# Two-layer hybrid decoder trunk: earlier weight sums, merge sums on VectorE, and first-layer Gram products and bonus later in program order

## The chip, the cores and the metric

The kernel runs on 1 core of one Trainium2 chip. The metric is device time in microseconds (us), one launch from start to end. Five engines take part: PE (TensorE, with PEld for its weight loads), DVE (VectorE), ACT (ScalarE), POOL (GpSimd) and SP, which only issues transfers. POOL and ACT also issue transfers from their own queues.

## The reference, cut to what matters

Two layers, each with a token mixer of three parallel branches merged by gates, and a gated MLP with a causal convolution of width 3. SEQ is 512, D_MODEL 1024, D_FF 2816.

```
h = rmsnorm(x, norm1_g[l]);  p = h @ w_in[l]
y_rw  = rwkv7_branch(...)       # 8 heads of 64, state recurrence, plus
                                # y + sum(r * k * r_k) * v       ("bonus")
y_ret = retention_branch(...);  y_sg = sgu_branch(...)
proj  = einsum('bsgc,gcd->bsgd', [y_rw, y_ret, y_sg], w_branch[l])
gates = sigmoid(gate_logits)                            # 3 branches
x = x + sum(gates * proj, axis=2) @ w_out[l]            # the merge
u = rmsnorm(x, norm2_g[l]) @ ffn_w_up[l]                # up projection
c = conv_b + sum_j conv_w[j] * shifted(u, j)
x = x + (silu(gate) * val) @ ffn_w_down[l]              # down projection
```

## The kernel before, in words

Activations lie transposed: a tile is 128 channels by 512 tokens. Every large product is made of three matmuls (`mm3`, L194). Each operand is split into a high part `hi` (a CAST by ACT) and a low part `lo` (a subtraction by DVE), and lo·hi, hi·hi and hi·lo are added up in one PSUM bank. Weights come as 128x512 tiles `wr` from DRAM through the SP queue and are split in `part`: ACT writes `wh` or `sh` (L175), DVE writes `wl` or `sl` (L178). The two names stand for two buffer pools and nothing else. `plan` is the list of weight tiles in the order of use, and `part` runs some tiles ahead of PE. PSUM has four banks `acc` for the large products and four banks `sm` for the rest.

The order of the instructions on each engine is set by a scheduler, which runs its own timeline over the program as written and its priorities. Only what goes through `keep_in_program_order` keeps the order written. So writing code elsewhere may or may not move instructions.

A layer runs in these stages:

- **RWKV columns and blocks.** `cols3(m)` makes the k, r and v columns of block m (two heads) by PE, then DVE (L594, L597) and ACT (L596). `prep(m)` makes decays and the tiles `X`, `Y`, `bk` of the block: two small products `wus` (L637, L638) into `sm` banks, a chain over ACT and DVE, and then the Gram products, 64 small matmuls (L676, L679) into four `sm` banks. ACT copies these banks out to `Y` (L681) and `GB` (L680). `bonus(m)` multiplies r, k and r_k, splits the result, sums it over a head with two matmuls by `bonesR` (L693, L694) into an `sm` bank, and multiplies with v (L695).
- **Solve and recurrence.** `solve` inverts triangular blocks on DVE (L890 to L910) while PE runs the gate columns (`fill`), then PE takes the result (L918). The recurrence over 8 chunks follows, also between gate columns.
- **Merges.** `SEQ` is the written order of the stage. `merge(l, br, m, ...)` fetches a gate tile `gth` from DRAM through the POOL queue (L1148), multiplies the branch's output with `w_branch` on PE (12 matmuls), and DVE computes (gate + 1) times product (L1151), which frees the `acc` bank. For the second branch in `SEQ` (`2`) the sum with the first branch's tile is done by POOL (L1154). For the last (`1`) it is done by DVE (L1154), followed by a split for `wout`.
- **FFN.** Up projections, 44 columns c of 24 matmuls per layer: PE, DVE (`fu`, L1202), ACT (`cv`, L1204), DVE (L1205, L1206), and for a pair Silu and a product (`fth`). The down projection uses sums and differences of quarters of the weights. They are formed beside the up projections: `presum(l, c)` goes through `PRE[l]`, a table from the first column `at` to the quadruple q. In columns at to at+3 it fetches four tiles `pre` (L289, SP queue), in columns at+4 to at+7 DVE forms one sum each (L162), and POOL's queue stores it (L304). The down projection starts while the last columns end.

Of the kernel before, what the change touches and what calls it, by code (L numbers as in the profile page):

```python
# [23 lines left out]
FIRST = (12, 4, 0, 8)  # L24
FILL = (36, 2, 1)
KEPT = 6
PRE = {0: {4 + 4 * k: 2 + k for k in range(9)}, 1: {4: 0, 10: 1, 16: 2, 22: 3, 29: 4, 36: 6}}
RSUM = {(0, 3): (0, 0), (0, 10): (0, 1), (1, 3): (1, 8), (1, 10): (1, 10)}
NOW = ((1, 5), (1, 7), (1, 9))
SEQ = "0 H G G 0 S 0 U U G G 0 S 0 0 S 2 2 Y 0 0 2 1 2 1 2 1 2 1 2 1 2 1 1 1"  # L30
# [23 lines left out]
class Emit:  # L54
# [109 lines left out]
    def part(self, u):  # L164
        raw, n, pool = self.raws.pop(0), u[4], u[5]
        if type(raw) is tuple:
            raw = self.sumnow(raw)

        self.turn = (self.turn + 1) % 5 if pool in ("p", "q") else 4
        if pool is None or self.turn < 3:  # L170
            hi, lo = [self.wp.tile([128, 512], F32R, name=self.nm(t), tag=t, bufs=3) for t in ("wh", "wl")]
        else:
            hi, lo = [{"f": self.f, "r": self.r, "u": self.u, "p": self.u, "q": self.u}[pool](dt=F32R, n=t) for t in ("sh", "sl")]
        with self.tc.high_priority() if pool in (None, "p", "q") else nullcontext():
            self.kept(self.nc.scalar.copy(hi[:, :n], raw[:, :n]))  # L175
            if self.raws and type(self.raws[0]) is tuple:
                self.sumnow(self.raws[0])
            self.kept(self.nc.vector.tensor_tensor(lo[:, :n], raw[:, :n], hi[:, :n], op=SUB))  # L178
        self.parts.append((hi, lo))
        self.npart += 1  # L180
# [102 lines left out]
    def presum(self, l, c):  # L283

        for at, q in PRE[l].items():
            n = c - at
            if 0 <= n < 4:
                self.pre[l, q, n] = t = (self.f if at < 21 else self.u if l or at in (28, 36) else self.r)(n="pre")
                self.kept(self.nc.sync.dma_start(t, self.raw4(l, q, (1, 3, 0, 2)[n])))  # L289
            if 4 <= n < 8:  # L290
                b = [self.pre[l, q, k] for k in (2, 0, 3, 1)]
                p = (7, 5, 6, 4)[n - 4]
                t, i = self.sum4(b, p)
                self.kept(i)
                self.stores.append(((l, q), p, t))
                self.store4(n=1)
# [188 lines left out]
    def mixer(self, l, nst):  # L485
# [15 lines left out]
        sg, out = self.sgu_v(l), self.rwkv_out(l, *st)  # L501
# [12 lines left out]
        for step in SEQ.split():  # L514
            if step == "S":
                self.ret_pair(*next(rows))
            elif step == "G":
                ysg.append(self.sgu_out(len(ysg)))
            elif step == "H":
                self.ret_heads()  # L520
            elif step == "U":
                next(rest), next(rest)
            elif step == "Y":
                yret = self.ret_out()
            elif step == "0":
                mg.append(self.merge(l, 0, len(mg), yrw))
            elif step == "2":
                mg[m2] = self.merge(l, 2, m2, ysg, mg[m2])
                m2 += 1
            else:  # L530
                out.append(self.split(self.merge(l, 1, len(out), yret, mg[len(out)], self.nc.vector), self.f))
        return out

    def fillers(self, l):
# [33 lines left out]
    def rwkv(self, l, nst):  # L568
# [53 lines left out]
        X, Y, BK, Vf, bv = [], [], [], [], []  # L622
        kc, rc = [], []

        def cols3(m):
            kc.append(col(4 + m))
            rc.append(col(m))
            Vf.append(col(8 + m))

        def prep(m):  # L630


            k, r, v = kc[m], rc[m], Vf[m]
            ms = slice(m * 128, m * 128 + 128)
# [33 lines left out]
            V.tensor_tensor(f, f, cx[:, 0:7, 64], op=MUL)  # L668
            V.transpose(tha, ksq)
            V.tensor_reduce(pr[:, m], tha.rearrange("p (j r) -> p j r", r=32), axis=AX.X, op=ADD)  # L670
            for g in range(2):
                pB, pK = [self.sm((128, 4, 128)) for _ in range(2)]
                for j in range(4):
                    c = 4 * g + j
                    for h in range(2):
                        i = T.matmul(pK[hv[1 - h], j, :], bk[hv[h], c, 1, :], x[hv[h], c, :], start=True, stop=True)  # L676
                        if c or h:
                            po(i)
                        po(T.matmul(pB[hv[h], j, :], bk[hv[h], c, 0, :], x[hv[h], c, :], start=True, stop=True))  # L679
                A.copy(GB[:, 8 * m + 4 * g:8 * m + 4 * g + 4, :], pB)  # L680
                A.copy(y[:, 4 * g:4 * g + 4, :], pK)  # L681
# [21 lines left out]
            self.pool = "p"  # L703
        cols3(1)
        self.pool = "p"
        prep(0)
        cols3(2)
        bonus(0)
        prep(1)
        cols3(3)  # L710
        bonus(1)
        prep(2)
        gd = col(13)
# [427 lines left out]
        return self.split(t2, self.f)  # L1141


    def merge(self, l, br, m, y, sum=None, add=None):

        nc = self.nc
        t = self.f(n="gth")
        nc.gpsimd.dma_start(t, self.gd[br, m])  # L1148
        ps = self.acc()
        self.matF(ps, ("wall", l, 58 + br * 4 + m // 2, m % 2 * 512), y)  # L1150
        nc.vector.scalar_tensor_tensor(t, t, 1.0, ps, op0=ADD, op1=MUL)  # L1151
        if sum is None:
            return t
        (add or nc.gpsimd).tensor_tensor(sum, sum, t, op=ADD)  # L1154
        return sum

    def wout(self, l, mg, xd, st):
# [566 lines left out]
```

## Time and profile before

| | |
|---|---|
| median of 3 runs | 1686.04 us (1684.36 to 1688.55) |
| profiled execution, its own time | 1686.46 us |
| its span, first to last instruction | 1684.7 us |
| outside the span | 1.8 us |
| granted TensorE clock over the span | 1.000 |
| PE idle inside the span | 1684.7 - 1673.6 = 11.1 us |

Stages by the trace: RWKV columns and blocks of the first layer run from about 25 to 125 us, its solve to about 200 us, the recurrence to 300 us, the merges from 360 to 464 us, the up projections to 738 us and the down projection after that. The second layer's merges run from 1200 to 1300 us, its up projections to 1577 us.

How to read the rows: a group or timeline row names the engine, the line of the kernel, the operation, output<-inputs, and in brackets the engine's idle time just before it with what ended it. Matmul durations overlap: a row of 0.39 us is followed by the next matmul 0.23 us later.

### The profile page before, as it was taken

To read this page: it belongs to the slowest core of one execution; us is meant where nothing else is said; L and a number is where in the kernel's file an instruction comes from. 1 tells how busy PE (TensorE), PEld (TensorE's weight loads), DVE (VectorE), ACT (ScalarE), POOL (GpSimd) and SP (SyncE) were. 2 spreads that over 40 slices of the span, in tenths; PEclk is the share of its full clock that TensorE was granted. 3 is DMA by queue.
4 is the path that set the end of the run, shared out by engine and by line. 5 is a ranking of instruction groups with operands and counts; after the bars stand their busy time and mean duration, and the time that the engine had idled before them with its cause. 6 is when DMAs were issued, how large, how long until landed. Compare 5 with 4: busy or idle time off the path is not lost.

```text
span 1684.7 us, 29297 instructions
## 1 busy us (share of the span) xinstructions
PE 1673.6 (99%) x10643; PEld 1392.5 (83%) x10643; DVE 1292.1 (77%) x2289; ACT 820.3 (49%) x1436; POOL 301.4 (18%) x450
## 2 busy tenths in 40 slices
PE   9999999999999999999999999999999999999998
PEld 7888877888888888889988887778888888888887
DVE  7887746578668888877868877565785688898897
ACT  6563433554254444456655634335542544444565
POOL 1121013312210111110111210233122012221100
PEclk9999999999999999999999999999999999999999
DMA  5236655533553666678733366655344436664775
GB/s 183 88 109 205 192 185 172 186 125 128 177 188 115 204 202 217 219 233 301 234 114 94 106 195 188 201 164 188 122 143 149 156 131 201 207 209 161 273 243 176
DMA packets 158592, 298.38 MB, mean 177 GB/s; under 512 B 21936, under 2 KB 32944, under 8 KB 158448
## 3 DMA queue, kind: packets, MB, share of 16 engines
q1 hardware_dynamic: 128864, 217.12, 40.2%
q0 software_dynamic: 21232, 64.25, 11.5%
q10 hardware_dynamic: 8352, 15.15, 2.5%
q8 instruction: 83, 1.36, 0.3%
q14 instruction: 61, 0.50, 0.1%
HBM read 236.40 MB, written 60.03 MB: 176 GB/s over the span
## 4 chain that ended last, share of the span: by engine, by line
PE 87%; DVE 5%; issue 3%; DMA 3%; ACT 1%; POOL 1%; SPq 1%; ACTq 0%; DVEq 0%; POOLq 0%
PE acc L194 75%; PE sm L194 5%; PE sm L769 2%; DMA wr<-wall 1%; PE sm L1025 1%; DVE sl L178 1%; PE sm L676 1%; DVE cv L1205 1%; DVE fu L1202 1%; SPq L726 1%; DVE cv L1206 1%; DMA tr<-vT 0%; DVE wl L178 0%; PE sm L1136 0%; ACT cv L1204 0%
## 5 line engine op out<-in xcount | busy, mean ns | idle before, releaser
L194 PE MATMUL acc<-lo,sh 128*128 128x512 f32 (+1 forms) x1144 | 443.0, 387 | 0.4 <-DVE gth L1151 0.4
L194 PE MATMUL acc<-hi,sh 128*128 128x512 f32 (+1 forms) x1144 | 441.8, 386 | 0.0
L194 PE MATMUL acc<-hi,sl 128*128 128x512 f32 (+1 forms) x1144 | 429.3, 386 | 0.5 <-DVE sl L178 0.5
L175 ACT CAST sh<-wr 128x512 fp32r<-128x512 f32 x352 | 212.2, 616 | 213.2 <-DMA wr<-wall 100.5
L175 ACT CAST wh<-wr 128x512 fp32r<-128x512 f32 x278 | 171.4, 620 | 270.8 <-PE acc L194 178.7
L178 DVE TENSOR_TENSOR wl<-wr,wh 128x512 fp32r<-128x512 f32 x278 | 196.2, 708 | 136.7 <-ACT wh L175 130.8
L178 DVE TENSOR_TENSOR sl<-wr,sh 128x512 fp32r<-128x512 f32 x352 | 239.9, 695 | 72.3 <-ACT sh L175 63.5
L194 PEld LDWEIGHTS acc<-lo,sh 128*128 128x128 f32 x1144 | 214.9, 188 | 45.1 <-issue 1.4
L194 PEld LDWEIGHTS acc<-hi,sl 128*128 128x128 f32 x1144 | 214.9, 188 | 44.1 <-DVE sl L178 0.9
L194 PEld LDWEIGHTS acc<-hi,sh 128*128 128x128 f32 x1144 | 214.9, 188 | 42.8
L194 PE MATMUL acc<-lo,wh 128*128 128x512 f32 (+1 forms) x636 | 245.1, 385 | 0.2 <-ACT wh L175 0.2
L194 PE MATMUL acc<-hi,wl 128*128 128x512 f32 (+1 forms) x636 | 243.3, 383 | 0.1
L194 PE MATMUL acc<-hi,wh 128*128 128x512 f32 (+1 forms) x636 | 242.5, 381 | 0.0
L1204 ACT ACTIVATE cv<-fu,pc 128x512 f32<-128x512 f32 x88 | 71.8, 816 | 175.1 <-DVE fu L1202 175.0
L194 PEld LDWEIGHTS acc<-hi,wl 128*128 128x128 f32 x636 | 119.6, 188 | 25.1 <-DVE wl L178 1.4
L194 PEld LDWEIGHTS acc<-lo,wh 128*128 128x128 f32 x636 | 119.6, 188 | 24.3 <-ACT wh L175 1.0
L194 PEld LDWEIGHTS acc<-hi,wh 128*128 128x128 f32 x636 | 119.7, 188 | 22.3 <-issue 0.2
L1205 DVE SCALAR_TENSOR_TENSOR cv<-fu,pc,cv 128x511 f32<-128x511 f32 x88 | 65.9, 748 | 30.2 <-ACT cv L1204 29.7
L194 PE MATMUL acc<-wl,hi 128*128 128x512 f32 x212 | 85.8, 405 | 0.0
L194 PE MATMUL acc<-wh,hi 128*128 128x512 f32 x212 | 82.5, 389 | 0.0
L194 PE MATMUL acc<-wh,lo 128*128 128x512 f32 x212 | 82.5, 389 | 0.0
L1202 DVE TENSOR_TENSOR fu<-acc,rsF 128x512 f32<-128x512 f32 x88 | 60.3, 685 | 14.2 <-PE acc L194 13.1
(423 smaller groups left out, 2605.4 us busy)
## 6 DMA issues: line engine op xcount, KB each, us to landing
wr<-wall SPq DMA_DIRECT2D x480, 256.0 KB, 3.0
wr<-ts SPq DMA_DIRECT2D x76, 256.0 KB, 4.4
wr<-wdt SPq DMA_DIRECT2D x66, 256.0 KB, 3.7
pre<-wdt SPq DMA_DIRECT2D x60, 256.0 KB, 3.6
ts<-pre POOLq DMA_DIRECT2D x60, 256.0 KB, 2.9
gd<-gth ACTq DMA_DIRECT2D x48, 256.0 KB, 2.6
gth<-gd POOLq DMA_DIRECT2D x48, 256.0 KB, 3.7
sp<-ab SPq DMA_DIRECT2D x22, 256.0 KB, 4.7
```

The costliest lines, as they stand in the source:

```text
L175: self.kept(self.nc.scalar.copy(hi[:, :n], raw[:, :n]))
L178: self.kept(self.nc.vector.tensor_tensor(lo[:, :n], raw[:, :n], hi[:, :n], op=SUB))
L194: i = self.nc.tensor.matmul(*x, **y, **kw)
L676: i = T.matmul(pK[hv[1 - h], j, :], bk[hv[h], c, 1, :], x[hv[h], c, :], start=True, stop=True)
L726: nc.sync.dma_start(o[r:r + 32, :].rearrange("d (e x) -> d e x", e=2), d[hv[h], j * n:j * n + n].rearrange("(e d) x -> d e x", d=32))
L769: po(T.matmul(o, l, r, start=start, stop=True, skip_group_check=True))
L1025: po(T.matmul(o, lhsT, rhs, start=start, stop=stop, skip_group_check=True))
L1202: V.tensor_tensor(u, ps, self.rsF, op=MUL)
L1204: A.activation(t, u, AF.Identity, scale=self.p("cw2", j), bias=self.p("cb", j))
L1205: V.scalar_tensor_tensor(t[:, 1:], u[:, :511], self.p("cw1", j), t[:, 1:], op0=MUL, op1=ADD)
L1206: V.scalar_tensor_tensor(t[:, 2:], u[:, :510], self.p("cw0", j), t[:, 2:], op0=MUL, op1=ADD)
```

## The change

Five edits:

1. `PRE`: nine quadruples of the first layer start at columns 4, 8, 12, 15, 19, 23, 26, 30, 34 instead of every fourth column up to 36. The last two of the second layer start at 28 and 34 instead of 29 and 36. The last sum so falls into column 41 instead of 43. The number of fetches, sums and stores stays.
2. `merge`: all sums are done by DVE; POOL's 8 per layer are gone from its queue.
3. `prep` becomes a generator `prepg` with a stop ahead of the Gram products. In the first layer, `cols3(2)` is written between the first half of block 0 and its Gram products; in the second layer nothing moves.
4. In the first layer, `bonus(0)` is written inside `cols3(3)`, behind its first column, instead of behind `cols3(2)`; `bonus(1)` stays behind `cols3(3)`.
5. The very first weight tile's CAST is written as two halves of 256 columns.

```
-PRE = {0: {4 + 4 * k: 2 + k for k in range(9)}, 1: {4: 0, 10: 1, 16: 2, 22: 3, 29: 4, 36: 6}}
+PRE = {0: {c: 2 + k for k, c in enumerate((4, 8, 12, 15, 19, 23, 26, 30, 34))}, 1: {4: 0, 10: 1, 16: 2, 22: 3, 28: 4, 34: 6}}
...
-            self.kept(self.nc.scalar.copy(hi[:, :n], raw[:, :n]))
+            for h in (slice(0, 256), slice(256, 512)) if self.npart == 0 and self.plan else (slice(0, n),):
+                self.kept(self.nc.scalar.copy(hi[:, h], raw[:, h]))
...
-                out.append(self.split(self.merge(l, 1, len(out), yret, mg[len(out)], self.nc.vector), self.f))
+                out.append(self.split(self.merge(l, 1, len(out), yret, mg[len(out)]), self.f))
...
-        def cols3(m):
+        def cols3(m, then=None):
             kc.append(col(4 + m))
+            if then:
+                then(0)
             rc.append(col(m))
             Vf.append(col(8 + m))
...
         def prep(m):
-
+            for _ in prepg(m):
+                pass
+
+        def prepg(m):
...
             V.tensor_reduce(pr[:, m], tha.rearrange("p (j r) -> p j r", r=32), axis=AX.X, op=ADD)
+            yield
             for g in range(2):
...
-        prep(0)
+        g0 = prepg(0)
+        next(g0)
+        if l:
+            next(g0, None)
         cols3(2)
-        bonus(0)
+        if l:
+            bonus(0)
+        else:
+            next(g0, None)
         prep(1)
-        cols3(3)
+        cols3(3, None if l else bonus)
         bonus(1)
...
-        (add or nc.gpsimd).tensor_tensor(sum, sum, t, op=ADD)
+        nc.vector.tensor_tensor(sum, sum, t, op=ADD)
```

Line numbers of the changed kernel are 1 to 13 higher than before. Three places show what the edits do to the order on an engine.

DVE at the end of the first layer's up projections, before (`pre` a sum of edit 1, `cv` the convolution of the last column, `sl` and `wl` low parts of weight tiles, `fth` the product behind Silu):

```order
L1202 TENSOR_TENSOR fu_7808<-acc_7771,rsF_5525 128x512
L178 TENSOR_TENSOR wl_7852<-wr_7726,wh_7851 128x512
L178 TENSOR_TENSOR wl_7870<-wr_7744,wh_7869 128x512
L1205 SCALAR_TENSOR_TENSOR cv_7810<-fu_7808,pc_176,cv_7810 128x511
L178 TENSOR_TENSOR wl_7888<-wr_7772,wh_7887 128x512
L1206 SCALAR_TENSOR_TENSOR cv_7810<-fu_7808,pc_176,cv_7810 128x510
L162 TENSOR_TENSOR pre_7594<-pre_7594,pre_7546 128x512
L178 TENSOR_TENSOR sl_7834<-wr_7720,sh_7833 128x512
L1214 SCALAR_TENSOR_TENSOR fth_7817<-fth_7817,cv_7810 128x512
```

The same engine and place after the change:

```order
L1215 TENSOR_TENSOR fu_7812<-acc_7775,rsF_5526 128x512
L179 TENSOR_TENSOR wl_7853<-wr_7733,wh_7852 128x512
L179 TENSOR_TENSOR wl_7871<-wr_7751,wh_7870 128x512
L1218 SCALAR_TENSOR_TENSOR cv_7814<-fu_7812,pc_177,cv_7814 128x511
L179 TENSOR_TENSOR wl_7889<-wr_7776,wh_7888 128x512
L1219 SCALAR_TENSOR_TENSOR cv_7814<-fu_7812,pc_177,cv_7814 128x510
L179 TENSOR_TENSOR sl_7835<-wr_7727,sh_7834 128x512
L1227 SCALAR_TENSOR_TENSOR fth_7818<-fth_7818,cv_7814 128x512
```

The sum ahead of `sl` is gone from this place, and the rest keeps its order.

POOL in the first layer's merges, before (`gth` written from `gd` is a fetch of a gate tile, `gth` from two `gth` a sum of edit 2):

```order
L1154 TENSOR_TENSOR gth_4520<-gth_4520,gth_4864 128x512
L1148 DMA gth_4914<-gd_2702 128x512
L1148 DMA gth_4937<-gd_1902 128x512
L1154 TENSOR_TENSOR gth_4670<-gth_4670,gth_4914 128x512
L1148 DMA gth_4964<-gd_2800 128x512
L1148 DMA gth_4987<-gd_1944 128x512
L1154 TENSOR_TENSOR gth_4692<-gth_4692,gth_4964 128x512
L1148 DMA gth_5014<-gd_1986 128x512
```

POOL in the same merges after the change:

```order
L1161 DMA gth_4915<-gd_2703 128x512
L1161 DMA gth_4938<-gd_1903 128x512
L1161 DMA gth_4965<-gd_2801 128x512
L1161 DMA gth_4988<-gd_1945 128x512
L1161 DMA gth_5015<-gd_1987 128x512
```

No sum stands between the fetches any more. On DVE each sum now stands one to three rows behind the product (L1151 before, L1164 after) that it adds.

PE behind the first layer's first Gram products (the row with `X` and `bk` is the last of them, `bonesR` marks a bonus, `wus` the small products of the next block), before:

```order
L679 MATMUL sm_607<-X_561,bk_563 64x128
L194 MATMUL acc_842<-hi_133,wh_676 128x512
L194 MATMUL acc_842<-hi_133,wl_677 128x512
L194 MATMUL acc_842<-lo_142,wh_676 128x512
L194 MATMUL acc_842<-hi_141,wh_676 128x512
L693 MATMUL sm_762<-lo_759,bonesR 128x512
L694 MATMUL sm_762<-hi_758,bonesR 128x512
L194 MATMUL acc_842<-hi_141,wl_677 128x512
L194 MATMUL acc_842<-lo_157,wh_694 128x512
L194 MATMUL acc_842<-hi_156,wh_694 128x512
L637 MATMUL sm_766<-lo_385,wus_235 128x512
```

PE at the same place after the change:

```order
L686 MATMUL sm_734<-X_562,bk_564 64x128
L195 MATMUL acc_834<-hi_134,wh_633 128x512
L195 MATMUL acc_834<-hi_134,wl_634 128x512
L195 MATMUL acc_834<-lo_143,wh_633 128x512
L195 MATMUL acc_834<-hi_142,wh_633 128x512
L643 MATMUL sm_758<-lo_386,wus_236 128x512
L644 MATMUL sm_758<-hi_385,wus_236 128x512
L195 MATMUL acc_834<-hi_142,wl_634 128x512
L195 MATMUL acc_834<-lo_158,wh_651 128x512
L195 MATMUL acc_834<-hi_157,wh_651 128x512
L643 MATMUL sm_759<-lo_393,wus_240 128x512
```

The first Gram products stand at the same place of PE's order in both kernels; the bonus has gone (to behind the second Gram products, beside `bonus(1)`), and block 1's first `wus` products have taken its place, five rows earlier than before. The third and fourth Gram products come 13 and 14 matmuls later than before.

More of the change, by code (lines that the diff above doesn't have):

```diff
@@ L287, in presum @@
             if 0 <= n < 4:
-                self.pre[l, q, n] = t = (self.f if at < 21 else self.u if l or at in (28, 36) else self.r)(n="pre")
+                self.pre[l, q, n] = t = (self.f if at < 20 else self.u if l or at in (26, 34) else self.r)(n="pre")
                 self.kept(self.nc.sync.dma_start(t, self.raw4(l, q, (1, 3, 0, 2)[n])))
@@ L1141, in sgu_out, with merge @@
         return self.split(t2, self.f)
-    def merge(self, l, br, m, y, sum=None, add=None):
+    def merge(self, l, br, m, y, sum=None):
         nc = self.nc
```

## The prediction, made before the changed kernel was run

> **What bounds the kernel now.** I read the page first (engines, clock), then the waits of PE, then the timeline at each place where PE waits.
>
> ```profile
> PE 1673.6 (99%) x10643; PEld 1392.5 (83%) x10643; DVE 1292.1 (77%) x2289; ACT 820.3 (49%) x1436; POOL 301.4 (18%) x450
> PEclk9999999999999999999999999999999999999999
> PE acc L194 <- DVE sl L178: 1.6, 2, 1.0
> PE sm L693 <- ACT Y L681: 0.5, 1, 0.5
> PE acc L194 <- DVE gth L1151: 0.4, 1, 0.4
> PE acc L194 <- DVE fu L1202: 0.3, 1, 0.3
> ```
>
> PE is busy for 1673.6 of 1684.7 us and the clock digit never drops. The change neither adds nor removes a matmul. So it can only win back PE's stalls or make new ones, and those beside the edits are few: 1.6 + 0.5 + 0.4 + 0.3 us in this list, and the start. These figures are idle time by modelled ends. The true loss at a place is the step from one matmul's start to the next, less the usual step (0.23 us for 512 columns, half of it, 0.12, for 256); that is what I use below.
>
> **The change part by part.**
>
> *Edit 1, no sums in the last columns.* The end of the first layer's up projections:
>
> ```profile
> 738.51 0.28 PE L194 MATMUL acc<-ah,sl 128*128 128x256 f32 x1
> 739.03 0.50 PE L194 MATMUL acc<-ah,sh 128*128 128x256 f32 x2 [0.24 <-ACT sh L175]
> 740.58 0.39 PE L194 MATMUL acc<-ah,sl 128*128 128x256 f32 x1 [1.04 <-DVE sl L178]
> 738.37 0.60 ACT L175 CAST sh<-wr 128x512 fp32r<-128x512 f32 x1
> 738.58 0.74 DVE L1206 SCALAR_TENSOR_TENSOR cv<-fu,pc,cv 128x510 f32<-128x510 f32 x1
> 739.24 0.69 DVE L162 TENSOR_TENSOR pre<-pre,pre 128x512 f32<-128x512 f32 x1
> 739.84 0.68 DVE L178 TENSOR_TENSOR sl<-wr,sh 128x512 fp32r<-128x512 f32 x1
> ```
>
> PE loses 739.03 - 738.51 - 0.12 = 0.40 us on `sh`, then 740.58 - 739.03 - 2 x 0.12 = 1.31 us on `sl`. The sum stands right ahead of this `sl` and starts one step, 0.60 us, before it (739.24 to 739.84); `sh` is done at 738.97. Without the sum `sl` starts at 739.24 and PE 0.60 us earlier. The 0.40 us hang on ACT's order, which stays, and the remaining 0.7 us on `cv`, which still stands ahead. I take 0.60, with bounds of 0 (other DVE work slides up) and 1.71 (both stalls gone, if the sums missing from the two columns before also let DVE run ahead).
>
> The end of the second layer's:
>
> ```profile
> 1574.13 0.61 PE L194 MATMUL acc<-wh,ah 128*128 128x512 f32 x2
> 1575.09 0.50 PE L194 MATMUL acc<-wl,ah 128*128 128x512 f32 x1 [0.34 <-DVE fu L1202]
> 1572.54 0.69 DVE L162 TENSOR_TENSOR pre<-pre,pre 128x512 f32<-128x512 f32 x1
> 1574.35 0.69 DVE L1202 TENSOR_TENSOR fu<-acc,rsF 128x512 f32<-128x512 f32 x1
> ```
>
> Here PE waits for a bank that `fu` frees, and loses 1575.09 - 1574.13 - 0.46 = 0.50 us. DVE works without a gap from the sum (1572.54) to `fu`, so without the sum `fu` ends 0.60 us earlier, and the whole 0.50 is gone. Bounds: 0 and 0.50. What is late next is the `sh` of the first layer's end; here nothing that the rows show.
>
> The sums are not removed but moved to earlier columns. In the first layer two columns (19 and 30) now hold two sums of 0.69 us, and two columns (15 and 26) fetch two `pre` tiles on SP's queue:
>
> ```profile
> 600.00:620.00 20.00, 20.00 (x90) 16.53 (x89) 17.56 (x32) 8.54 (x15) 3.24 (x6) 1.00 0.69 226
> 660.00:680.00 20.00, 20.00 (x90) 16.57 (x89) 17.84 (x32) 8.60 (x16) 2.70 (x5) 1.00 0.56 190
> POOL ts L304 <- DVE pre L162: 193.2, 52, 7.4
> ```
>
> In these windows DVE (third figure) is idle for 2.4 and 2.2 us of 20, PE not at all, so a column of 5.4 us has 0.6 us of slack and the second sum takes it up over two columns. Only POOL's store waits for a sum, 193.2 us in total, and nobody hangs on that. Cost 0, at most 2 x 0.69 = 1.4 us if the slack can't be used.
>
> *Edit 2, merge sums on DVE.*
>
> ```profile
> L1154 POOL TENSOR_TENSOR gth<-gth,gth x16: 1277/1294/1676, 402.3 to 1287.4; 128x512 f32<-128x512 f32 x16
> L1154 DVE TENSOR_TENSOR gth<-gth,gth x16: 682/692/1295, 418.7 to 1297.1; 128x512 f32<-128x512 f32 x16
> 443.01 1.28 POOL L1154 TENSOR_TENSOR gth<-gth,gth 128x512 f32<-128x512 f32 x1 [3.43 <-DVE gth L1151]
> 444.25 1.08 POOL L1148 DMA_DIRECT2D gth<-gd  x2
> 448.59 0.69 DVE L1151 SCALAR_TENSOR_TENSOR gth<-gth,acc 128x512 f32<-128x512 f32 x1 [0.37 <-DMA gth<-gd]
> 448.59 0.39 PE L194 MATMUL acc<-hi,sl 128*128 128x512 f32 x1
> 449.42 0.47 PE L194 MATMUL acc<-lo,sh 128*128 128x512 f32 x1 [0.45 <-DVE gth L1151]
> 443.41 1.44 DVE L178 TENSOR_TENSOR sl<-wr,sh 128x512 fp32r<-128x512 f32 x1 [0.48 <-PE acc L194]
> 449.48 1.71 DVE L178 TENSOR_TENSOR sl<-wr,sh 128x512 fp32r<-128x512 f32 x1 [0.21 <-ACT sh L175]
> 440.00:464.00 24.00, 23.55 (x104) 19.22 (x103) 15.53 (x21) 5.39 (x9) 4.63 (x6) 1.00 0.50 166
> ```
>
> DVE gets 16 x 0.69 = 11.1 us, 5.5 per layer, off PE's path: in the last window it is idle for 8.5 of 24 us, and four to five sums fall into it (3 us). DVE also gets time back: the two `sl` of 443.41 and 449.48, which ran beside a POOL sum, took 1.44 and 1.71 instead of 0.69. PE's one stall of this stage costs 449.42 - 448.59 - 0.23 = 0.60 us. PE waits for a bank, the product L1151 frees it, and that product waited for a gate tile whose fetch stood on POOL's queue behind the sum of 443.01. Without the sum the fetch is issued up to 1.28 us earlier, more than the stall. I take 0.60 off; bounds 0.60 off and 0.69 on (one more DVE sum just ahead of a product that PE waits for).
>
> *Edits 3 and 4, first layer.*
>
> ```profile
> 67.15 0.40 PE L194 MATMUL acc<-hi,wh 128*128 128x512 f32 x1
> 68.00 0.50 PE L693 MATMUL sm<-lo,bonesR 128*128 128x512 f32 x1 [0.46 <-ACT Y L681]
> 66.85 0.62 ACT L175 CAST sh<-wr 128x512 fp32r<-128x512 f32 x1 [1.94 <-DMA wr<-wall]
> 67.37 0.58 ACT L681 COPY Y<-sm 128x512 f32<-128x512 f32 x1
> 184.11 2.29 DVE L903 STREAM_TRANSPOSE cs<-cs 128x512 f32<-128x512 f32 x2
> L918 PE MATMUL sm<-cs,GB x256: 190/192/213, 196.5 to 1037.0; 32*32 32x32 f32 x128
> ```
>
> PE loses 68.00 - 67.15 - 0.23 = 0.62 us at the first bonus. It waits there for an `sm` bank, and the bank for ACT's copy at 67.37, which stands behind a CAST that waits for a weight tile. By the order of the changed kernel the Gram products stand where they stood, ACT's CAST and copies follow in the same order, and in place of the bonus comes `wus`, which needs an `sm` bank too. So the stall changes its name and stays: I take 0, bounds 0.62 off (another bank is free) and 0.6 on (it gets the bank of the next copy, 0.48 us later). The later Gram products of blocks 2 and 3 (14 x 0.23 = 3.2 us) push the solve: its last transposes before PE's products end at 186.4 and PE takes them at 196.5, so 10 us cover it. If that cover were gone, up to 3.2 us would show.
>
> *Edit 5, the first CAST in halves.*
>
> ```profile
> 4.43 0.62 ACT L175 CAST wh<-wr 128x512 fp32r<-128x512 f32 x1 [0.53 <-DMA wr<-wk]
> 6.42 0.72 ACT L260 ACTIVATE hi<-x,x0g 128x512 fp32r<-128x512 f32 x1 [1.37 <-DMA x<-xT]
> 8.05 0.19 PEld L194 LDWEIGHTS acc<-lo,wh 128*128 128x128 f32 x1 [0.37 <-ACT wh L175]
> 741.16 0.41 ACT L1240 CAST ah<-fth 128x256 fp32r<-128x256 f32 x1 [2.19 <-DVE fth L1214]
> ```
>
> A CAST of 256 columns takes 0.41 us, so PE could start 0.21 us earlier. But its second group of products is held until 8.05 by a chain that begins with the transfer of the second x tile, which ACT awaits at 6.42. The gain is lost there: 0, bounds 0.21 off and 0.
>
> **Sum:** 0.60 + 0.50 + 0.60 = 1.7 us off. From the profiled execution, 1686.46, that gives 1684.8; it lies 0.4 us above the median of the three runs, 1686.04, from which it gives 1684.3. I take 1684.5.
>
> **The rivals.**
>
> *Nothing comes of it.* The freed 0.6 us steps are filled by the next operation in DVE's order, as the scheduler reorders 88% full stretches: 1686.0. For it speaks that DVE at the two ends has `cv` and other `sl` and `wl` queued closely; against it, that the order listed for the first layer's end keeps the same rows without the sum.
>
> *All stalls near the edits go:* 1.71 + 0.50 + 0.60 + 0.62 + 0.21 = 3.6 us off, 1682.4. Against it speak the same bank and the same ACT order at 68.00.
>
> *DVE becomes the bound in the merges, slower.* Two merges take PE 24 x 0.23 = 5.5 us; DVE then has two products, two sums, two or three `sl` and a `lo`, up to eight operations of 0.60 us steps, 4.8 us. Above nine it decides: each of eight pairs would lose a step of 0.6 us, 4.8 us in the second branch's merges of both layers and as much again if banks come late, 1686 + 4.8 to 9.6, in the middle 1693. Against it speak the idle 8.5 us of 24. The Trainium skill's page "SBUF", section "Who interferes with whom", says that a DVE instruction with two SBUF inputs and a GpSimd instruction that reads SBUF hold a shared port, whichever comes first blocking the other for its whole length; the rows 1.44 and 1.71, which end 0.56 us after the POOL sums' ends, agree. By that rule no such block is left in the merges, so the 16 sums come partly out of time that DVE lost before, which lowers this rival's chance. The sum itself goes by the rows alone.
>
> *The shifted solve shows:* 3.2 us on less 1.7 off, 1687.5; against it the 10 us.
>
> **How the numbers follow.** Forecast (1 to 2.5 us off) 0.47, nothing 0.27, all stalls gone 0.11, solve or another small new stall 0.11, DVE bound in the merges 0.04. The range runs from 1681.8 (all gone, with the spread of the runs, 1684.36 to 1688.55, allowing some 0.6 more) to 1688.0 (small new stalls of up to 2 us). 0.3% of 1686 is 5.1 us, about what a measurement can tell from no change. The largest gain of the rivals is 3.6, so faster by more has 0.04, from the spread of medians alone. Slower by more needs DVE as the bound or several solve-like shifts: 0.05.
>
> **What would show it.** Right: the row at 740.58 with a wait 0.6 us shorter, no wait for `fu` near 1575, no wait for `gth` in the merges, and a wait of 0.5 us for ACT's `Y` now on `wus` at about 68. POOL's L1154 group is gone and DVE's has 32 of 0.69 us, without the 1.295. Wrong: new PE waits for `sl` in columns 19 to 21 or 30 to 32, waits for `gth` in both layers' merges, or a PE wait for DVE at L918.

## The result and the profile after

The changed kernel takes 1692.44 us in the median of five runs (1690.20 to 1694.97); the kernel before, in the five runs that stand beside it, 1687.17 (1684.36 to 1688.55). The ratio is 1.0032, with a 95% interval of 1.0021 to 1.0043: slower by 5.3 us, where 1.7 us less were forecast. The profiled execution took 1691.71 us, its span is 1690.0, 5.3 us over the span of before.

First the engines from the page of the changed kernel, and then from its list of PE's waits:

```profile
PE 1674.7 (99%) x10643; PEld 1393.4 (82%) x10643; DVE 1293.4 (77%) x2305; ACT 819.9 (49%) x1437; POOL 280.1 (17%) x434
```

```profile
PE acc L195 <- DVE gth L1164: 3.2, 2, 1.9
PE sm L782 <- ACT U L820: 2.1, 1, 2.1
PE acc L195 <- ACT sh L176: 0.6, 2, 0.3
PE sm L643 <- ACT Y L688: 0.5, 1, 0.5
PE acc L195 <- DVE sl L179: 0.4, 1, 0.4
```

PE does the same work in the same time, DVE hardly more (POOL's 16 sums are gone, 301 to 280 us). Two entries stand out: the wait for the merges' products (`gth`) has grown from one of 0.4 us to two of together 3.2 us, and one of 2.1 us for the copy of U in the solve is new. Of the two waits for `sl`, 1.6 us, one of 0.4 us is left, and the 0.3 us for `fu` are gone.

**The solve.** The second step of the first layer's solve in the timeline, before and then after:

```profile
225.22 0.38 SPq L135 DMA_DIRECT2D wr<-wall  x1
226.15 0.22 PE L769 MATMUL sm<-Vt,bk 64*64 64x64 f32 x1
228.52 0.33 ACTq L553 DMA_DIRECT2D gd<-gth  x1
228.89 0.37 ACT L807 COPY U<-sm 128x256 f32<-128x256 f32 x1 [2.21 <-DMA wr<-wall]
```

```profile
227.09 0.80 SPq L739 DMA_DIRECT2D bkS<-tr  x2
227.98 1.45 SPq L135 DMA_DIRECT2D wr<-wall  x1
227.44 0.22 PE L782 MATMUL sm<-Vt,bk 64*64 64x64 f32 x1
231.93 0.33 ACTq L554 DMA_DIRECT2D gd<-gth  x1
232.30 0.37 ACT L820 COPY U<-sm 128x256 f32<-128x256 f32 x1 [4.33 <-DMA wr<-wall]
232.72 0.27 PE L782 MATMUL sm<-U,GB 64*64 64x64 f32 x1 [2.14 <-ACT U L820]
```

The two transfers in the chain of waits after (start, length, what):

```profile
222.28 4.74 DMA tr<-bkT
227.98 3.87 DMA wr<-wall
```

The copy of U has its input when PE's products end (226.15, 227.44), but on ACT it stands behind the store `gd<-gth`. That store's own tile is ready at 227.97; in the program's list, in both kernels, it also waits for a DMA completion counter, and it goes out at 231.93, 0.08 us after the weight load has landed (227.98 + 3.87). The load stands on SP's queue behind `bkS<-tr`, the fetches of a transposed ("turned") tile of the solve, which wait until that tile has landed in DRAM at 222.28 + 4.74 = 227.02. So the copy followed the start of the last product by 2.74 us before and by 4.86 us now, while PE has fill work for about 2.7 us in between (twelve steps of 0.23). Before, the cover was used up already.

**The merges.** The chain of waits of the changed kernel, second layer, 1275 to 1290 us, in order of time (start, length, what):

```profile
1274.80 9.85 PE acc L195 x44
1284.64 1.57 issue
1286.21 0.63 ACT sh L176
1286.84 0.02 issue
1286.86 0.69 DVE sl L179
1287.56 0.61 DVE gth L1164
1288.16 0.14 issue
1288.30 1.83 PE acc L195 x7
```

PE needs a bank; the product `gth` frees it; on DVE the product stands behind an `sl`; that `sl` waits for `sh`, and `sh` waits for PE by the program's list (it takes a buffer that products of PE have read; the profile shows no releaser, "issue"). The same turn stands in the first layer, where PE's stall ends at 448.21. There the order of DVE's instructions in the kernel before is (names with numbers: tile and buffer)

```
576 L1154 TENSOR_TENSOR gth_4418<-gth_4418,gth_4887
577 L187 TENSOR_TENSOR lo_4911<-gth_4418,hi_4910
578 L178 TENSOR_TENSOR sl_5074<-wr_5017,sh_5073
579 L1151 SCALAR_TENSOR_TENSOR gth_4914<-gth_4914,acc_4916
580 L178 TENSOR_TENSOR sl_5092<-wr_5044,sh_5091
581 L1151 SCALAR_TENSOR_TENSOR gth_4937<-gth_4937,acc_4939
```

and the changed kernel (its numbers are one higher)

```
583 L179 TENSOR_TENSOR sl_5075<-wr_5018,sh_5074
584 L188 TENSOR_TENSOR lo_4912<-gth_4419,hi_4911
585 L179 TENSOR_TENSOR sl_5093<-wr_5045,sh_5092
586 L1164 SCALAR_TENSOR_TENSOR gth_4915<-gth_4915,acc_4917
587 L1164 SCALAR_TENSOR_TENSOR gth_4938<-gth_4938,acc_4940
588 L1167 TENSOR_TENSOR gth_4671<-gth_4671,gth_4915
```

One `sl`, ten weight tiles ahead, has moved in front of the product of acc 4917 (4916 before). The bank of that product is the one that the merge four later needs. In this first-layer place the `sl` waits for PE itself, since its own buffer was last read by a product just ahead of the stall. PE, `sl` and product now take turns with no overlap.

**Where the 5.3 us are.** I set each matmul's start against the same matmul of before; the table has the growth of that difference between places (times of before, us), for the changed kernel and for six of the runs told below. The row 752 to 1225 holds the second layer's start and solve; no edit of these kernels touches it, and it swings from -1.0 to +3.3 us between executions. So one profile's total is good to about 2 us either way, but a single place with a named wait can be read more closely. Even there `before` is one execution: the -0.6 to -0.8 us in the row of the first layer's merges stand in kernels with and without edit 2, for its stall at 449 is mostly absent from the others.

| stretch | changed | e1_pre | e2_merge | e3_gram | h1_qpool | h3_pairs | f2_all |
|---|---|---|---|---|---|---|---|
| 0 to 140 (start, columns, bonuses) | 0.67 | 0.37 | 0.10 | 1.26 | 0.33 | 0.13 | 1.04 |
| 140 to 195 | 0.56 | 0.00 | 0.00 | 0.59 | 0.00 | 1.58 | 0.00 |
| 195 to 246 (first solve steps) | 2.16 | -0.05 | -0.05 | 1.63 | -0.05 | -0.04 | -0.05 |
| 246 to 475 (merges, layer 0) | 0.82 | -0.59 | 0.82 | 0.38 | -0.66 | -0.83 | -0.79 |
| 475 to 752 (up projections) | -0.59 | -0.32 | 0.00 | 0.00 | 0.01 | 0.00 | -0.59 |
| 752 to 1225 | -0.02 | 1.03 | 1.80 | 0.22 | -1.03 | 0.51 | 3.31 |
| 1225 to 1470 (merges, layer 1) | 2.58 | 0.29 | 2.05 | -0.14 | 0.17 | 0.63 | -0.19 |
| 1470 to end | -0.89 | -0.89 | -0.03 | 0.04 | -0.09 | -0.03 | -0.84 |
| sum | 5.29 | -0.16 | 4.69 | 3.98 | -1.32 | 1.98 | 1.89 |

### The profile page after: what moved, and what is told of

Read it like the earlier page. It is cut to its first block, busy times and chain, and to the rows that moved or that the text cites. A ratio compares the mean times of both kernels' runs of the same rounds, so it can differ in the third digit from the quotient of the medians.

```text
span 1690.0 us, 29280 instructions
## 1 busy us (share of the span) xinstructions
PE 1674.7 (99%) x10643; PEld 1393.4 (82%) x10643; DVE 1293.4 (77%) x2305; ACT 819.9 (49%) x1437; POOL 280.1 (17%) x434
## 4 chain that ended last, share of the span: by engine, by line
PE 88%; DVE 6%; DMA 2%; issue 2%; ACT 1%; POOL 0%; SPq 0%; DVEq 0%; ACTq 0%; POOLq 0%
PE acc L195 77%; PE sm L195 5%; PE sm L782 2%; DMA wr<-wall 1%; DVE sl L179 1%; PE sm L1038 1%; DVE cv L1219 1%; DVE cv L1218 1%; DVE fu L1215 1%; PE sm L683 1%; PE sm L1149 0%; ACT cv L1217 0%; DVE ah L188 0%; DVE fth L1227 0%; DMA tr<-bkT 0%
## 5 line engine op out<-in xcount | busy, mean ns | idle before, releaser
L176 ACT CAST wh<-wr 128x512 fp32r<-128x512 f32 (+1 forms) x279 | 171.4, 619 | 267.2 <-PE acc L195 173.4
```

Of the source, the lines that this page charges most:

```text
L176: self.kept(self.nc.scalar.copy(hi[:, h], raw[:, h]))
```

## The experiments

Each is timed against the kernel before on the same chip, mostly in eleven runs; times are medians, ratios carry their 95% interval. The hypothesis after the comparison: two new waits, one by DVE's order in the merges, one by the later solve. The rivals: slow transfers of that one execution, the work of the sums itself, the split cast.

### Each edit by itself

Edit 1 alone (`PRE` and the choice of pools from the diff, nothing else):

> The kernel before with edit 1 alone (the tables of the sums). By the ledger of PE's steps the changed kernel won at these places what was forecast: 0.7 us at the end of the first layer's up projections (1.31 to 0.60 us at the row near 744) and 0.5 us for fu near 1575. If the edits add, this kernel is 1.1 to 1.5 us faster than before (0.07 to 0.09%), and none of the new stalls (the solve near 232, the merges near 448 and 1288) is in its profile. Rival: the missing sums let VectorE run ahead and a stall comes up elsewhere in the second layer's FFN (0.27 us near 1468): then 0.5 us or nothing.

1686.55 us against 1687.13; 0.9995 (0.9986 to 1.0004). The profile has the shortened `sl` wait (0.61 us at 739.99) and no `fu` wait; the gain at the two ends is 0.32 + 0.89 us by the table. At the two waits it is as expected by size, but 0.28 us are lost again on `sh` just ahead of that `sl`; in time it is too small to be told from nothing.

Edit 2 alone:

```diff
-        (add or nc.gpsimd).tensor_tensor(sum, sum, t, op=ADD)
+        nc.vector.tensor_tensor(sum, sum, t, op=ADD)
```

> The kernel before with edit 2 alone (all merge sums on VectorE). Theory: without POOL's sums VectorE's order of instructions is another one, in which the third pair's product stands behind an sl that waits for a buffer; PE loses about 1.5 us there in the first layer and 2.1 us in the second, against 0.60 us won at the stall near 449 and 0.67 us in each layer where POOL's sum held up vt near 405 and 1244: 1.5 to 2.7 us slower in all (0.09 to 0.16%). Rival: the stalls of 448 and 1288 came from the later arrival of PE at the merges (edits 3 and 4 shifted it by 3.4 us) or from one execution's transfers: then this kernel is 1.9 us faster than before.

1690.84 against 1687.13; 1.0022 (1.0013 to 1.0031). The waits for `gth` are there without edits 3 and 4, and to the digit as in the changed kernel (list of PE's waits):

```profile
PE acc L194 <- DVE gth L1151: 3.2, 2, 1.9
```

By its steps PE loses 1.47 us at 444.85 and 2.10 us at 1287.36, in the changed kernel 1.47 and 2.10 as well. A fixed order repeats like that; a slow transfer of one execution would not. The rival is out.

Edits 3 and 4 alone (`prepg`, `cols3` and the calls from the diff):

> The kernel before with edits 3 and 4 alone (first layer's first Gram products behind the next columns, bonus behind one more). Theory: the whole solve comes later; its transposed tiles come back later on SP's queue, the weight transfer queued behind them lands later, ACT's store of a gate tile waits for that transfer and the copy of U stands behind the store: PE waits about 2.2 us for U near 231, and 0.4 us are lost at the bonuses: 2.2 to 2.8 us slower (0.13 to 0.17%). Rival: the 2.2 us were this one execution's slow transfers (4.74 and 3.87 us instead of some 4.0 and 3.3); the order itself costs only 0.8 us: 0.8 to 1.2 us slower, with a wait for U near 231 of about 0.8 us.

1689.71 against 1687.13; 1.0013 (1.0005 to 1.0022). PE waits for U at 232.82 again and loses 1.56 us, in the changed kernel 2.30: the wait comes with the edit. Its size goes with PE's own lateness: the copy of U starts at 232.39 here and at 232.30 there, but PE comes to it 0.8 us later here.

Edit 5 alone, and the changed kernel without edit 5:

```diff
-            self.kept(self.nc.scalar.copy(hi[:, :n], raw[:, :n]))
+            for h in (slice(0, 256), slice(256, 512)) if self.npart == 0 and self.plan else (slice(0, n),):
+                self.kept(self.nc.scalar.copy(hi[:, h], raw[:, h]))
```

> The kernel before with edit 5 alone (first cast in halves). In the changed kernel's profile PE ran its first ten products at the slow step of 0.43 us until 5.5 us, the kernel before only until 4.2 us, and that left the start 0.9 us later. Theory: the moment at which the step changes is of the execution, not of the edit, so this kernel takes as long as before, within 0.3 us, and its profile may show the change of the step at either time. Rival: the halved cast delays the start: 0.6 to 0.9 us slower, with the change of the step at 5.5 us again.

> The changed kernel without edit 5 (the first cast whole). Theory: edit 5 costs nothing, its 1.4 us alone are the spread of the second layer's start and of the moment at which PE's step changes; then this kernel is as slow as the changed one, ratio to before 1.0028 to 1.0040. Rival: the split costs 1.4 us by itself; then 1.0020 to 1.0026.

Alone 1.0008 (0.9999 to 1.0017), left out 1.0043 (1.0030 to 1.0056) where the whole change has 1.0032 (1.0021 to 1.0043). Alone it is 1.5 us over before instead of the 0.3 us that were expected, but the interval holds 1; without it the loss is no smaller. Both numbers together leave no cost of the split that could be told. In the profile of edit 5 alone most of the extra time lies at the second layer's start (2.7 us more in 1000 to 1030), where the order of the instructions is that of before.

Edit 3 without edit 4 (`bonus(0)` stays behind the third columns, ahead of the first Gram products):

> Edit 3 without edit 4: the first Gram products behind the next columns, the bonus where it was before. Theory: the later Gram products carry the loss, since the solve hangs on them: PE waits for U near 232 for 1 us or more, 1.5 to 2.2 us slower than before. Rival: the bonus moved into the fourth columns takes the sm banks from the later Gram products and so makes the solve late; then the wait for U is under 0.4 us here and the kernel within 0.6 us of before.

1693.40 against 1686.61; 1.0039 (1.0026 to 1.0051), worse than both edits together. Here the bonus stands in front of the Gram products, and the solve comes later still: PE waits 1.8 us for `XB` near 220 and 1.1 us for U, and loses 1.0 us on `wh` at 169. Both expectations missed by size. The direction, that a later solve costs more, holds, but 3.0 us of this profile's loss lie between 140 and 195 us, ahead of the solve's results, and are not explained by it.

### The merges: order or work?

Edit 2 with order kept in all merges:

```diff
+        self.keep = True
         self.matF(ps, ("wall", l, 58 + br * 4 + m // 2, m % 2 * 512), y)
-        nc.vector.scalar_tensor_tensor(t, t, 1.0, ps, op0=ADD, op1=MUL)
+        self.kept(nc.vector.scalar_tensor_tensor(t, t, 1.0, ps, op0=ADD, op1=MUL))
+        self.keep = False
```

> Edit 2 alone (all merge sums on VectorE), but in the merges the weights' casts, the sl and the products keep the order in which the program writes them, so that no sl for a weight tile six and more merges ahead stands in front of a product. Theory (VectorE's order): the two stalls of edit 2 alone, 1.47 us near 445 and 2.10 us near 1287, are gone; what edit 2 wins stays (0.60 us near 449 and 0.67 us in each layer at vt), so this kernel is 1.3 to 1.9 us faster than before (0.08 to 0.11%), against 3.7 us slower of edit 2 alone. Rival: it is the work of the 16 sums on VectorE that makes the products late, or the gate tiles' fetches; then PE still waits for gth in both layers, 1 us and more each, and the kernel is at least 2 us slower than before.

1689.51 against 1686.61; 1.0016 (1.0007 to 1.0025). No wait for `gth` is left, as the theory said, but the forecast gain did not come. In the first branch's merges, which have no sum, the kept order makes PE late at products with `sl` (0.30 and 0.23 us at 375 and 378, the same at 1216 and 1218). That is 1.1 us; the rest of the 2.7 us by which this kernel is slower is not explained by a wait in the merges.

So the order is kept only where something is added (`self.keep = sum is not None`):

> Edit 2 alone with the program's order of casts, sl and products kept only in the merges that add to a sum (the second and third branch), and not in the first branch's. With the order kept in all merges the two stalls for gth went, but PE waited for sl in the first branch, 0.5 us twice in each layer, 0.85 us net. Theory: those waits came from the kept order in the first branch; here they are gone too, and only edit 2's wins are left: 1.0 to 1.9 us faster than before. Rival: the sums on VectorE cost time by themselves; then 1 us or more slower than before.

1687.04 against 1686.55; 1.0001 (0.9992 to 1.0010). PE's waits in full:

```profile
PE acc L194 <- DVE sl L178: 1.6, 2, 1.0
PE acc L423 <- DVE rst L420: 1.5, 1, 1.5
PE sm L769 <- ACT U L807: 0.8, 1, 0.8
PE sm L693 <- ACT Y L681: 0.5, 1, 0.5
PE sm L769 <- DVE s L831: 0.4, 2, 0.2
PE sm L676 <- issue: 0.4, 1, 0.4
PE acc L194 <- DVE fu L1202: 0.3, 1, 0.3
PE acc L194 <- ACT sh L175: 0.2, 1, 0.2
```

The sums are the same 32 on DVE, and the 3.7 us of edit 2 are gone. Their work costs nothing that can be told; their order did. The gain of 1.0 to 1.9 us that I expected on top is not measured. The table's 0.83 us in the first layer's merges are no sign of it: the kernels with POOL's sums in place have 0.59 (edit 1 alone) and 0.66 there (edits 3 and 4 with POOL's fetches).

### The solve: whose lateness?

Edits 3 and 4 with the first layer's gate stores on POOL's queue (`(self.nc.scalar if l else self.nc.gpsimd).dma_start(d, t)`):

> Edits 3 and 4 alone, and the first layer's stores of gate tiles issued by POOL instead of ACT, so that on ACT the copy of U no longer stands behind a store that waits for an earlier transfer's counter. Theory (the copy of U waits behind the store): PE's wait for U near 232 falls from 1.56 us to under 0.4 us, and the kernel is 0.5 to 1.0 us slower than before instead of 2.2 us. Rival (the solve itself comes too late): U's matmuls upstream are late by 3 us, the wait near 232 stays at 1 us or more, and the time stays about 2 us over before.

1697.57 against 1686.61; 1.0066 (1.0053 to 1.0079). A miss that taught something: the wait for U is gone, but a weight load sits behind fetches of turned tiles on SP's queue until 243.9 and takes 5.9 us, and PE waits 4.5 us for S at 252. The edit also dealt the completion counters out anew over the transfers; whether that is why the load comes so late is not shown.

Edits 3 and 4 with U copied by DVE in that one step (`(V.tensor_copy if c == 1 and not l else A.copy)(U, P1[:, 1])`):

> Edits 3 and 4 alone, and in the first layer's second solve step the copy of U is done by VectorE instead of ACT; the stores, their counters and SP's queue stay as they are. Theory (the copy stands behind a store on ACT that waits for a late weight transfer): VectorE copies U within 1 us of PE's product instead of 4.1 us, PE's wait for U near 232 is gone (1.56 us to under 0.2 us), and the kernel is 0.3 to 1.0 us slower than before instead of 2.2 us. Rival (the weight itself is late): PE then waits at the same place for wl or wh of the late weight tile, 1 us or more, and the time stays 2 us over before.

1687.87 against 1687.11; 1.0008 (0.9999 to 1.0017). U is copied at once, and PE then waits for S, the next result of the step (timeline):

```profile
227.80 0.42 DVE L819 COPY U<-sm 128x256 f32<-128x256 f32 x1
233.53 0.69 DVE L178 TENSOR_TENSOR wl<-wr,wh 128x512 fp32r<-128x512 f32 x1 [5.31 <-ACT wh L175]
234.59 0.42 DVE L831 TENSOR_TENSOR S<-S,F 128x256 f32<-128x256 f32 x1
235.16 0.65 PE L781 MATMUL sm<-S,X 64*64 64x64 f32 x29 [1.09 <-DVE S L831]
```

DVE sat 5.31 us in front of the `wl` of the late tile, with S behind it. The copy was only the first in line; the late weight tile is behind both, so the rival was half right.

Edits 3 and 4 with the fetches of turned tiles in the solve steps on POOL's queue, off SP's:

```diff
-        def turn(o, d, head):
+        def turn(o, d, head, q=nc.sync):
-                    nc.sync.dma_start(o[r:r + 32, :]...
+                    q.dma_start(o[r:r + 32, :]...
-                turn(o[:, 256 * a:...], d[:, 256 * a:...], lambda h: h ^ a)
+                turn(o[:, 256 * a:...], d[:, 256 * a:...], lambda h: h ^ a, nc.gpsimd if g and not l else nc.sync)
```

> Edits 3 and 4 alone, and the first layer's solve fetches its turned tiles in the solve steps (the bkS tiles of the second half) on POOL's queue instead of SP's, so that the weight tiles on SP's queue no longer stand behind fetches that wait for a transfer. Theory (the weight tile is late because it is queued behind those fetches): in the stretch of 215 to 245 PE loses no more than before (1.8 to 1.9 us by its steps, against 3.2 us), with no wait for U or S over 0.4 us, and the kernel is 0 to 1.0 us slower than before instead of 2.2 us. Rival (the solve's own tiles are late, whatever the queue): PE waits for U, S or XB there for 1 us or more. Risk: POOL issues a fetch in 0.54 us against SP's 0.43, and the sixteen fetches may come too late for the fourth step.

1687.27 against 1686.55; 0.9999 (0.9990 to 1.0008). PE's waits in full:

```profile
PE acc L194 <- DVE sl L178: 1.6, 2, 1.0
PE acc L423 <- DVE rst L420: 1.5, 1, 1.5
PE sm L781 <- DVE s L843: 0.4, 2, 0.2
PE sm L642 <- ACT Y L687: 0.4, 1, 0.4
PE acc L194 <- ACT sh L175: 0.4, 2, 0.2
PE acc L194 <- DVE fu L1214: 0.3, 1, 0.3
```

No U, no S. The Gram products are as late as before this repair, and the weights come in time; the load behind the first turned tile goes out at 223.28 instead of 228.31, and the copy of U at 227.47 instead of 232.39 (the later times are those of edits 3 and 4 alone; timeline of this run):

```profile
223.28 0.33 SPq L135 DMA_DIRECT2D wr<-wall  x1
227.47 0.37 ACT L819 COPY U<-sm 128x256 f32<-128x256 f32 x1 [0.40 <-ACT gth L551]
```

With the run before it, in which S came late though U did not, that leaves one root: the weight tile behind the fetches on SP's queue.

### Both together, and versions that might win

The changed kernel with the first repairs of both (order kept in all merges, U by DVE), and then with the roots repaired (order kept in the adding merges, fetches on POOL's queue), all five edits in place:

> The changed kernel with both new waits taken away: casts, sl and products in the program's order in the merges, and the copy of U in the first layer's second solve step on VectorE. If the two waits are what made the changed kernel slower, 2.2 us at U and 0.8 to 2.3 us in the merges (as the two repairs gave alone), it is at 1.0005 to 1.0016 of before instead of 1.0032, and its profile has no wait for gth and none for U in the first layer. Rival: something else in the changed kernel (edit 5, the second layer's output projection) holds the loss: 1.0020 or more.

> The changed kernel, all five edits, with both roots repaired: order kept in the adding merges, and the first layer's fetches of turned tiles in the solve steps on POOL's queue. If VectorE's order in the merges and SP's queue in the solve are the whole of the loss, this kernel is no slower than the repaired parts: 1.3 us faster (edit 1 with the kept sums, 0.9991) plus 0 (edits 3 and 4 on POOL's queue, 0.9999), so 0.9988 to 0.9996 instead of 1.0032, with no wait for gth, and none for U over 0.3 us in the first layer. Rival: what is left of the changed kernel costs by itself (bonuses, first cast): 1.0005 or more.

1.0013 (1.0003 to 1.0023) and 0.9996 (0.9987 to 1.0005), where the changed kernel has 1.0032. With the two roots gone nothing of the loss is left that can be told. By their ratios the parts also add up: 3.7 us for edit 2 and 2.2 for edits 3 and 4, less 0.8 for edit 1, are 5.1 of the 5.4 us. The profile of the second has no wait for `gth` and none for U in the first layer; its 1.2 us for U are in the second layer, which the repair leaves alone.

Three versions without edits 3 to 5: edit 1 with order kept in all merges; edit 1 with U by DVE in both layers; edit 1 with order kept in the adding merges.

> A version that may beat both: edit 1 (the tables of the sums) and the merge sums on VectorE with the products kept in the program's order, the first layer and the first cast as before. If the two add, 0.8 + 1.3 to 1.9 us, it is 2.1 to 2.7 us faster than before (ratio 0.9984 to 0.9988). Rival: a new wait comes up where the two meet in the second layer's output projection; then under 1 us faster.

> A version that may beat both: edit 1 alone and, in both layers, the second solve step's copy of U on VectorE. Before, PE waits 0.2 us for U in the first layer and, by the execution, 0.1 to 0.9 us in the second. If the gains add: 0.8 + 0.3 to 1.0 us, 1.1 to 1.8 us faster than before (0.9989 to 0.9993). Rival: the copy on VectorE delays a wl that PE needs in the solve; then no faster than edit 1 alone (0.9995).

> Edit 1 and the merge sums on VectorE with the order kept in the adding merges only: the version with the most in it that the single runs let hope for. If the gains add, 0.8 + 1.0 to 1.9 us, it is 1.8 to 2.7 us faster than before (0.9984 to 0.9989). Rival: no faster than edit 1 alone (0.9995).

1.0004 (0.9995 to 1.0013), 0.9996 (0.9987 to 1.0005) and 0.9991 (0.9983 to 1.0000). All three expectations were too hopeful. The third, 1685.77 us against 1686.55, has the lowest ratio of all runs. Its interval just touches 1.

The third with the solve's fetches on POOL's queue in both layers:

> Edit 1, the merge sums on VectorE with the order kept in the adding merges, and in both layers the solve steps' fetches on POOL's queue; first layer and first cast as before. The second layer's wait for U (0.1 to 0.9 us by the execution) should go as well: 1.5 us of the version without it and 0.3 to 0.7 us, ratio 0.9986 to 0.9990. Rival: POOL's slower issues come too late in the second layer: then no better than 0.9991.

1688.31 against 1687.88; 1.0005 (0.9996 to 1.0014). The rival's time came, but by another mechanism: PE waits twice, 1.6 us each by its steps, for S at 1095 and 1107 in the second layer, and the last fetch of a turned tile is issued at 1071, well before. S stands on DVE behind instructions that wait for other work of POOL: first a tile `cs` of a weight sum that its queue fetches, then its `rs` (timeline):

```profile
1092.57 0.69 DVE L162 TENSOR_TENSOR cs<-cs 128x512 f32<-128x512 f32 x1 [5.41 <-DMA cs<-wdt]
1104.49 0.69 DVE L840 TENSOR_TENSOR y<-y,rs 128x512 f32<-128x512 f32 x1 [4.68 <-POOL rs L839]
```

How the moved fetches make these late is not shown.

## Why the prediction was wrong

**Edit 1: right.** The forecast took 0.60 us off the last `sl` and 0.50 off `fu`. The same place after:

```profile
743.24 0.50 PE L195 MATMUL acc<-ah,sh 128*128 128x256 f32 x2 [0.24 <-ACT sh L176]
744.19 0.39 PE L195 MATMUL acc<-ah,sl 128*128 128x256 f32 x1 [0.44 <-DVE sl L179]
1575.62 0.68 DVE L1215 TENSOR_TENSOR fu<-acc,rsF 128x512 f32<-128x512 f32 x1
```

744.19 - 743.24 - 0.24 = 0.71 us instead of 1.31: 0.60 less. For `fu` PE has no wait any more. The double sums in columns 19 and 30 show no wait, as forecast.

**Edit 2: wrong.** The step that failed is "I take 0.60 off; bounds 0.60 off and 0.69 on". The stall at 449 did go, and the fetches came earlier, by more than was said. Its price was one execution's, though: in the nine profiles that keep POOL's sums this place costs 0.60, 0.05, 1.03, 0, 0.18, 0.04, 0, 0 and 0.46 us, 0.26 in the mean, and nothing in the ten with edit 2. And the upper bound was the length of one more DVE operation. The place was priced by what DVE has to do, and the order in which it does it was not followed. An instruction that moves in front of another on an in-order engine brings its own wait with it, and that wait was for PE itself. The measured price is 1.47 + 2.10 us. The rival "DVE becomes the bound" was not it either: DVE was idle while PE waited (1.4 us ahead of the `sl` at 1286.86).

The Trainium skill's page "SBUF — State Buffer", section "Who interferes with whom", lets a DVE operation with two SBUF inputs and a POOL operation that reads SBUF exclude each other, and this trace agrees. In the group view the small `vt` products, before and after:

```profile
L1076 DVE SCALAR_TENSOR_TENSOR vt<-ry,rrr,vt x32: 337/346/1382, 393.7 to 1246.7; 128x128 f32<-128x128 f32 x32
L1089 DVE SCALAR_TENSOR_TENSOR vt<-ry,rrr,vt x32: 342/343/347, 397.3 to 1247.6; 128x128 f32<-128x128 f32 x32
```

Their longest falls from 1382 to 347 ns. PE gains nothing by it: it starts its products 3.39 us later than before ahead of this place (405 us) and 3.37 us later behind it (413 us). The 0.67 us that the expectations above put there for each layer are not in the trace.

**Edits 3 and 4: wrong.** The step is "10 us cover it". The cover was read at the first place where the solve meets PE. The second step had none: its copy of U came 2.74 us after the product with 2.7 us of fill work. The rival "the shifted solve shows", given 0.11 with the other small stalls and priced at up to 3.2 us on, is one that came, with 2.2 us. What I named of SP's queue was the number of its loads; that the weight loads stand behind the solve's fetches, and an ACT store behind a weight load, was not followed. The stall at 68 did move from the bonus to `wus` as forecast (0.62 to 0.63 us).

**Edit 5: right**, as far as it can be told.

**The chances.** The kernel's slack was read as an average (DVE idle 8.5 of 24 us, 10 us of cover), and so only small losses were thought possible; slower by over 0.3% had 0.05. Two losses, of 3.7 and 2.2 us by their ratios, were enough.

## What to carry to other kernels

When a change moves work between engines, follow the new order on each in-order queue up to the instruction that frees the bottleneck's buffer, and ask for what the instruction ahead of it waits. Idle time on an engine is no slack while something that waits stands first in its queue. A stall read in one profile is worth its size only if other executions show it too. Cover has to be read at every meeting point of a shifted chain; the tightest decides, and one with a wait of some tenths already has none.

## What was not expected of the hardware

PE's first products run at about half its usual rate, a step of 0.43 us instead of 0.23, and when that ends differs by execution. The last six of the ten products ahead of the kernel's work, before and then in the run of edit 1 alone:

```profile
3.39 1.98 PE L423 MATMUL acc<-rst 128*128 128x256 f32 x6
3.39 2.77 PE L423 MATMUL acc<-rst 128*128 128x256 f32 x6
```

Over all profiles of this study the step falls from 0.43 to 0.23 us somewhere between 4.2 and 7.7 us, and the 40th full product (512 columns) starts between 14.4 and 15.6 us, with the split cast and without. The kernel before has the earliest change; it puts the changed kernel 0.8 us behind at 12 us, of which 0.3 us are left at 60 us (the kernel before has small waits there that the late one hasn't), and no edit is behind that.

The half rate can also come back after a wait. In the run of the changed kernel without edit 5, at the stall in the second layer's merges:

```profile
1287.62 0.39 PE L194 MATMUL acc<-hi,sl 128*128 128x512 f32 x1
1289.95 0.58 PE L194 MATMUL acc<-lo,sh 128*128 128x512 f32 x1 [1.94 <-DVE gth L1163]
1290.33 0.63 PE L194 MATMUL acc<-hi,sh 128*128 128x512 f32 x1
1290.75 0.63 PE L194 MATMUL acc<-hi,sl 128*128 128x512 f32 x1
```

After 2.33 us between two starts, 1.94 of them idle, seven steps are 0.43 us, 1.4 us lost on top. In the changed kernel's own profile the same gap has no such stretch behind it. Seven and six such steps stand in two more profiles, soon after a step of 1.99 us at 220.33 (edit 3 without edit 4) and after one of 4.91 us at 252.19 (gate stores on POOL's queue). Of the eleven runs of edit 2 alone, three show a mean granted clock of 0.998 and took 1692.9 us on average, the other eight (0.999 and 1.000) 1690.1; so, as an estimate from these means, a kernel with such stalls may lose some 2.8 us more, by the execution; that the half rate is behind it is not shown for these runs. The Trainium skill's page "TensorE: Matmul & The Clock Gate", section "Part 1: The HAM clock gate (the "warmup" mystery)", tells of a half-rate state that ends after a busy window whose phase is free. A spread at the start agrees with that, but the page gives 4 us of activity, with 0.5 us either way, and here the step falls 2.7 to 6.2 us after the first product. It puts the return to half rate after an idle window of about 3.4 us, and here 1.9 us of idle time were enough.
